# First MLP product with the two parts of an activation factor side by side in one matmul

## The chip, the cores and the metric

The kernel runs on one core of a Trainium2 chip. The metric is the device time of one execution in microseconds. Five engines work side by side, each through its own queue in order: TensorE (PE, with weight loads shown as PEld), VectorE (DVE), ScalarE (ACT), GpSimd (POOL) and SyncE (SP, which here only starts DMAs).

## What is computed

One residual layer on 512 frames of 2048 channels, all in fp32: an input projection, stick-breaking attention, a spatial gating unit, a gated merge, an output projection, and then the MLP:

```python
    for l in range(DEPTH):
        ...
        merged = jax.nn.sigmoid(gate_a) * y_a + jax.nn.sigmoid(gate_b) * y_b
        x = x + merged @ w_out[l]

        h2 = rms_norm(x, g_ff[l])
        x = x + jnp.square(jax.nn.relu(h2 @ w_ff1[l])) @ w_ff2[l]
    return x
```

The change is in `h2 @ w_ff1`, which is 512 x 2048 by 2048 x 8192.

## The kernel before

**Precision.** Each fp32 operand is split into a rounded part `hi` and a remainder `lo`, both in a format that TensorE takes in one pass. A product is the sum of three matmuls: hi by hi, hi by lo, and lo by hi (`mm3`, lines 69 to 73). `split_to` makes the parts: ACT writes hi (line 106), DVE subtracts it from the source (line 107).

**The first MLP product.** The 8192 columns go in 32 pairs of blocks of 128 columns. The first two pairs are computed plainly (bank `f`). The other 30 go through `hidden` and `strassen_columns`, which needs seven products instead of eight: y11, y21, m7, m6, y22, m4, m5. A product is 8 steps of 256 rows of the contraction, and each step is one `mm3` with 256 columns (half of the frames). Its stationary operand is a combination of weight blocks, made in `Sums.parts`: DVE sums at lines 173 (for m7), 177 (m6), 179 (y22); a GpSimd DMA that adds into a buffer at line 175 (m5). Its moving operand is one of the activation factors `hs[name, k]`, a 512-wide tile with hi in its left half and lo in its right half, held in SBUF for all pairs.

**Buffers.** The parts of a product's weights, `w_hi` and `w_lo`, are in six pieces (line 156), so those of three products fit. The products share PSUM banks of 512 columns, of which only the left 256 are used: bank 0 takes y11, then m6 on top of it, then m5 on top; bank 1 y21; bank 2 m7, then m4; bank 3 y22. Each product that goes on in a bank needs what stood there to have been read first. `slot` hands out 64 tiles of 512 columns for everything else.

**Evictions.** `evac` in `hidden` builds the four quarters a11, a12, a21, a22 of the pair's result in two `relu` tiles: ACT writes the first term of each from PSUM (y11, m7, m6, y22; line 773), DVE adds the others (y21, m4 and twice m5; line 776). Then ACT applies the ReLU (line 780), and `keep_hidden` squares (line 686), forms the factors of the second product on DVE (`m`, lines 693 to 696), splits them (`ys`) and stores them to DRAM (line 700). The second MLP product (`strassen_tokens`) reads them back.

**Order.** The code is written product by product, but a scheduler fixes each engine's order when the program is built: on every engine instructions of one product stand between those of others. On PE the products of a pair run as y11, y21, m7, y22, m6, m4, m5, before the change and after it.

Of the kernel before, what the change touches and what calls it, by code (L numbers as in the profile page):

```python
# [12 lines left out]
ALU = mybir.AluOpType  # L13
# [21 lines left out]
def tile_hybrid_layer(ctx: ExitStack, tc: tile.TileContext, x, g_mix, w_in, g_q, g_k, ln_g, ln_b,  # L35
# [4 lines left out]
    nc = tc.nc  # L40
# [12 lines left out]
    def slot(name, dt=F32, pool=slots):  # L53
        return pool.tile([P, 512], dt, name=name, tag="slot")

    def acc(name):
        return ps_acc.tile([P, 512], F32, name=name, tag="acc")
# [11 lines left out]
    def mm3(o, lh, rh, start, stop, **kw):  # L69

        nc.tensor.matmul(o, lhsT=lh[0], rhs=rh[0], start=start, stop=False, **kw)  # L71
        nc.tensor.matmul(o, lhsT=lh[0], rhs=rh[1], start=False, stop=False, **kw)  # L72
        nc.tensor.matmul(o, lhsT=lh[1], rhs=rh[0], start=False, stop=stop, **kw)  # L73
# [4 lines left out]
    def step():  # L78
        if behind:
            behind.popleft()()  # L80
# [5 lines left out]
    def weight(wap, kt, c0, w=W):  # L86

        ck = CK * W // w
        raw = state["raw"].tile([P, ck, w], F32, name="w_raw", tag="w_raw")
        state["load"] = nc.sync.dma_start(  # L90
            out=raw, in_=wap[kt * P:(kt + ck) * P, c0:c0 + w].rearrange("(k p) c -> p k c", p=P))
        hi = wpool.tile([P, ck, w], F32R, name="w_hi", tag="w_piece", bufs=6)
        nc.scalar.copy(out=hi, in_=raw)  # L93
        lo = wpool.tile([P, ck, w], F32R, name="w_lo", tag="w_piece", bufs=6)
        nc.vector.tensor_tensor(out=lo, in0=raw, in1=f32(hi), op=ALU.subtract)  # L95
        return hi, lo

    def split(src, name, scale=None, pool=slots):

        hi, lo = slot(name + "_hi", F32R, pool), slot(name + "_lo", F32R, pool)  # L100
        split_to(hi, lo, src, scale)
        return hi, lo
# [47 lines left out]
    HS = S // 2  # L150
# [38 lines left out]
    def strassen_columns(wap, c0, rhs, evac, loaded=True):  # L189

        KH = KT // 2
        blocks = {(h, c): wap[:, c0 + c * P:c0 + (c + 1) * P].rearrange("(k h p) c -> h p k c", p=P, h=2)[h]
                  for h in range(2) for c in range(2)}
        w = Sums(blocks, [state["raw"].tile([P, KH, P], F32, name="w_raw", tag="w_raw") for _ in range(6)],
                 loaded)
        banks = {}
        for name in NAMES:
            hi, lo = w.parts(name)
            b, new = BANK[name]
            if new:  # L200
                banks[b] = acc("q")
            o = banks[b][:, :HS]
            for k in range(KH):
                mm3(o, (hi[:, k, :], lo[:, k, :]), rhs[name][k], new and k == 0, k == KH - 1,
                    skip_group_check=True)
            evac(name, o)
            step()

    def strassen_tokens(wap, r0, c0, lhs, evac, between, loaded=True, after=None):
# [243 lines left out]
    for half in range(2):  # L453
# [4 lines left out]
                 lambda tb, o, v=v: v.append(split(o, "v", rstd[:, tb:tb + 1])), "v")  # L458
# [82 lines left out]
    with tc.issue_after(ref.ins):  # L541
        ws, bs = [], []
        for half in range(2):
            t = slot("ws")
            nc.sync.dma_start(out=t.rearrange("p (g j) -> p g j", g=4),
                              in_=w_sp[0, half * 4:half * 4 + 4].rearrange("g i j -> i g j"))
# [117 lines left out]
    def sides(t):  # L664
        return t[:, :HS], t[:, HS:]

    hs = {}
    order = []
    for b in range(KT):
        y = x2T[b]  # L670
        with tc.issue_after(order[b - 2].ins) if b > 1 else nullcontext():
            nc.vector.tensor_tensor(out=y, in0=y, in1=rstd_b, op=ALU.mult)
        for half in range(2):
            name = "y" + "12"[b % 2] + "12"[half]
            far = name == "y11" or name == "y21" and b // 2 < LONG - KT // 2
# [46 lines left out]
    for p in range(PLAIN):  # L722
        o = [acc("f1") for _ in range(2)]
        for kt in range(0, KT, 4):
            hi, lo = weight(w_ff1[0], kt, p * 2 * P, 2 * P)
# [3 lines left out]
            for c in range(2):  # L729
                for k in range(4):  # L730
                    a = [part[:, k, c * P:(c + 1) * P] for part in (hi, lo)]
                    for half in range(2):
                        name = "y" + "12"[k % 2] + "12"[half]
# [12 lines left out]
    class Late:  # L746
# [3 lines left out]
            self.name = name  # L750

        def __getitem__(self, k):
            return sides(hs[self.name, k])

    rhs = {name: Late(name) for name in NAMES}
    last_factors(0)
# [8 lines left out]
    def hidden(p):  # L765

        act = [slot("relu"), slot("relu")]
        a11, a12, a21, a22 = (act[c][:, half * HS:(half + 1) * HS] for c in range(2) for half in range(2))

        def evac(name, o):  # L770
            for a, sign in {"y11": [(a11, 1.0)], "m7": [(a22, 1.0)], "m6": [(a21, -1.0)],
                            "y22": [(a12, 1.0)]}.get(name, []):
                nc.scalar.activation(out=a, in_=o, func=AF.Copy, scale=sign)
            for a, op in {"y21": [(a11, ALU.add)], "m4": [(a21, ALU.add)],
                          "m5": [(a22, ALU.subtract), (a12, ALU.add)]}.get(name, []):
                state["evac"] = nc.vector.tensor_tensor(out=a, in0=a, in1=o, op=op)

        strassen_columns(w_ff1[0], p * 2 * P, rhs, evac, loaded=p < pairs - 1)
        for a in act:
            nc.scalar.activation(out=a, in_=a, func=AF.Relu)  # L780
        return act
# [11 lines left out]
    for p in range(PLAIN, pairs - 1):  # L793
        acts.append(hidden(p))
        flush()
        for _ in range(min(len(acts), 1 if p == PLAIN else 2)):
            keep_hidden(p + 1 - len(acts), acts.pop(0))
    act = hidden(pairs - 1)

    def residual(half, t, c):  # L800
# [84 lines left out]
```

## Time and profile before

| what | value |
|---|---|
| time, median of 3 runs | 2509.46 us (2508.89 to 2510.39) |
| span of the profiled execution | 2507.8 us |
| instructions in it | 35108 |
| mean granted TensorE clock | 0.997 |
| 256-column matmuls of `strassen_columns` | 3 x 1680 |
| their stretch of the span | from about 1270 to 1840 us |
| pairs in that stretch | 30 |

The profiled execution shows no time of its own beside its span. In the page's rows a group has its line, engine and operation, the tiles it writes and reads, its shape and count, the busy time and the mean duration of one, and the idle time in front of it with the instruction that ended it. In a timeline the first column is the start in us, the second the duration.

### The profile page before, as it was taken

Reading aid. Unit: us, or ns where it says so; the run is one execution under the profiler, and the core shown is the slowest. Engines: PE = TensorE matmul, PEld = TensorE weight load, DVE = VectorE, ACT = ScalarE, POOL = GpSimd, SP = SyncE. Lnnn points to the kernel's source line nnn. Section 1 sums busy time; section 2 is a strip of 40 time slices with the busy share of each in tenths; the row PEclk is TensorE's granted clock in tenths of the full one; section 3 lists DMA queues with packets and bytes.
Section 4 is the critical chain, followed back from the end, with each engine's and each line's share of the span. In section 5 each row is a group of like instructions: output and inputs, shape, how many; then the busy total and the mean of one; then the engine's idle time right before and its main releaser. Section 6 shows DMA issues by size and latency. Waiting matters only on the chain.

```text
span 2507.8 us, 35108 instructions
## 1 busy us (share of the span) xinstructions
PE 2477.8 (99%) x13658; PEld 2163.2 (86%) x13658; DVE 1603.1 (64%) x2111; ACT 1034.0 (41%) x1510; POOL 329.5 (13%) x420
## 2 busy tenths in 40 slices
PE   8999999999999999999999999999998999999999
PEld 7888888888888888888899999999996888888887
DVE  4556463223334343332698888888878989889887
ACT  5333342222322322232366666666663443333333
POOL 0212110000121010100000000000023223212210
PEclk9999999999999999999999999999999999999999
DMA  5322322333333234344269888888888887767763
GB/s 177 92 85 74 87 75 91 94 101 93 118 93 109 93 93 126 110 146 141 92 155 256 220 227 224 228 224 220 224 277 322 257 282 239 233 219 217 249 181 94
DMA packets 322584, 416.01 MB, mean 166 GB/s; under 512 B 16960, under 2 KB 176752, under 8 KB 322416
## 3 DMA queue, kind: packets, MB, share of 16 engines
q1 hardware_dynamic: 265440, 320.94, 40.1%
q0 software_dynamic: 56976, 92.82, 15.4%
q8 instruction: 107, 1.75, 0.3%
q14 instruction: 61, 0.50, 0.1%
HBM read 346.58 MB, written 67.11 MB: 165 GB/s over the span
## 4 chain that ended last, share of the span: by engine, by line
PE 94%; DMA 2%; DVE 2%; issue 1%; ACT 1%; POOL 0%; SPq 0%; DVEq 0%; POOLq 0%
PE q L72 17%; PE q L73 16%; PE q L71 16%; PE xo L73 2%; PE xo L71 2%; PE xo L72 2%; PE gb L71 2%; PE gb L73 2%; PE gb L72 2%; PE ga L71 2%; PE ga L72 2%; PE ga L73 2%; DMA w_raw<-in_w_ff_dram 1%; PE v L71 1%; PE v L73 1%; PE v L72 1%
## 5 line engine op out<-in xcount | busy, mean ns | idle before, releaser
L106 ACT CAST w_hi<-w_raw 128x1024 fp32r<-128x1024 f32 x434 | 456.7, 1052 | 586.6 <-PE q L72 536.7
L95 DVE TENSOR_TENSOR w_lo<-w_raw,w_hi 128x1024 fp32r<-128x1024 f32 x216 | 268.1, 1241 | 595.6 <-ACT w_hi L93 591.4
L107 DVE TENSOR_TENSOR w_lo<-w_raw,w_hi 128x1024 fp32r<-128x1024 f32 x434 | 530.2, 1223 | 128.1 <-ACT w_hi L106 128.1
L93 ACT CAST w_hi<-w_raw 128x1024 fp32r<-128x1024 f32 x216 | 226.6, 1049 | 663.2 <-PE ga L72 99.6
L71 PE MATMUL q<-ys,w_hi 128*128 128x256 f32 x1680 | 474.0, 283 | 0.8 <-ACT w_hi L106 0.8
L72 PE MATMUL q<-ys,w_hi 128*128 128x256 f32 x1680 | 473.9, 283 | 0.0
L73 PE MATMUL q<-ys,w_lo 128*128 128x256 f32 x1680 | 469.9, 283 | 0.0
L72 PE MATMUL q<-w_lo,ys 128*128 128x512 f32 x896 | 350.5, 391 | 10.7 <-DVE w_lo L107 10.7
L73 PE MATMUL q<-w_hi,ys 128*128 128x512 f32 x896 | 349.8, 390 | 0.0
L71 PEld LDWEIGHTS q<-ys,w_hi 128*128 128x128 f32 x1680 | 322.5, 192 | 1.0 <-ACT w_hi L106 1.0
L72 PEld LDWEIGHTS q<-ys,w_hi 128*128 128x128 f32 x1680 | 322.5, 192 | 0.0
L73 PEld LDWEIGHTS q<-ys,w_lo 128*128 128x128 f32 x1680 | 320.1, 192 | 0.0
L71 PE MATMUL q<-w_hi,ys 128*128 128x512 f32 x896 | 313.7, 390 | 0.3 <-DVE x L832 0.3
L72 PEld LDWEIGHTS q<-w_lo,ys 128*128 128x128 f32 x896 | 168.9, 189 | 47.9 <-DVE w_lo L107 13.0
L71 PEld LDWEIGHTS q<-w_hi,ys 128*128 128x128 f32 x896 | 168.5, 188 | 35.8 <-DVE x L832 0.7
L73 PEld LDWEIGHTS q<-w_hi,ys 128*128 128x128 f32 x896 | 168.9, 189 | 34.9
L175 POOL DMA_DIRECT2D w_raw<-in_w_ff_dram x57 | 79.4, 1393 | 773.7 <-DVE w_raw L173 461.3
L832 DVE TENSOR_TENSOR x<-x,q 128x512 f32<-128x512 f32 x256 | 168.0, 682 | 5.8 <-PE q L73 4.1
L788 POOL DMA_DIRECT2D ys<-store x224 | 124.6, 566 | 244.9 <-PE q L73 186.8
L71 PE MATMUL xo<-w_hi,mT_hi 128*128 128x512 f32 x256 | 100.5, 393 | 0.0
L73 PE MATMUL xo<-w_hi,mT_lo 128*128 128x512 f32 x256 | 99.9, 391 | 0.0
L72 PE MATMUL xo<-w_lo,mT_hi 128*128 128x512 f32 x256 | 99.7, 389 | 0.0
(259 smaller groups left out, 4220.6 us busy)
## 6 DMA issues: line engine op xcount, KB each, us to landing
w_raw<-in_w_ff_dram SPq DMA_DIRECT2D x256, 512.0 KB, 5.0
w_raw<-in_w_in_dram SPq DMA_DIRECT2D x144, 512.0 KB, 3.8
store<-ys SPq DMA_DIRECT2D x224, 256.0 KB, 5.0
ys<-store POOLq DMA_DIRECT2D x224, 256.0 KB, 6.1
w_raw<-in_w_ff_dram POOLq DMA_DIRECT2D x57, 512.0 KB, 6.9
w_raw<-in_w_out_dram SPq DMA_DIRECT2D x32, 512.0 KB, 3.7
w_raw<-in_w_oa_dram SPq DMA_DIRECT2D x16, 512.0 KB, 3.6
w_raw<-in_w_ob_dram SPq DMA_DIRECT2D x16, 512.0 KB, 3.7
```

Source lines behind the costliest of these rows:

```text
L71: nc.tensor.matmul(o, lhsT=lh[0], rhs=rh[0], start=start, stop=False, **kw)
L72: nc.tensor.matmul(o, lhsT=lh[0], rhs=rh[1], start=False, stop=False, **kw)
L73: nc.tensor.matmul(o, lhsT=lh[1], rhs=rh[0], start=False, stop=stop, **kw)
L93: nc.scalar.copy(out=hi, in_=raw)
L95: nc.vector.tensor_tensor(out=lo, in0=raw, in1=f32(hi), op=ALU.subtract)
L106: nc.scalar.copy(out=hi, in_=src)
L107: state["lo"] = nc.vector.tensor_tensor(out=lo, in0=src, in1=f32(hi), op=ALU.subtract)
L175: nc.gpsimd.dma_start(out=self.w21, in_=self.blocks[1, 1], accum_op=ALU.add)
L788: nc.gpsimd.dma_start(out=f32(t), in_=store[f][NAMES.index(name), p])
L832: nc.vector.tensor_tensor(out=a, in0=a, in1=o, op=op)
```

## The change

`strassen_columns` no longer calls `mm3`. A step has two matmuls: w_hi by the whole tile (hi and lo side by side, 512 columns), and w_lo by its left half (256 columns). The left half of the bank then holds hi by hi plus lo by hi, the right half hi by lo. `evac` gets the right half as `far`. ACT copies it to a `cross` tile in SBUF after every product, and GpSimd combines these copies and adds them to the quarters: eight operations of 128x256 a pair. Since a bank runs on from y11 to m6 to m5, the right half of m6's copy has y11's in it; the GpSimd steps for m4 and m5 allow for that.

```diff
-            o = banks[b][:, :HS]
+            o = banks[b]
             for k in range(KH):
-                mm3(o, (hi[:, k, :], lo[:, k, :]), rhs[name][k], new and k == 0, k == KH - 1,
-                    skip_group_check=True)
-            evac(name, o)
+                y = rhs[name][k]
+                nc.tensor.matmul(o, lhsT=hi[:, k, :], rhs=y, start=new and k == 0, stop=False,
+                                 skip_group_check=True)
+                nc.tensor.matmul(o[:, :HS], lhsT=lo[:, k, :], rhs=y[:, :HS], start=False, stop=k == KH - 1,
+                                 skip_group_check=True)
+            evac(name, o[:, :HS], o[:, HS:])
...
-        def evac(name, o):
+        cross = {}
+
+        def evac(name, o, far):
             for a, sign in {"y11": [(a11, 1.0)], "m7": [(a22, 1.0)], "m6": [(a21, -1.0)],
                             "y22": [(a12, 1.0)]}.get(name, []):
                 nc.scalar.activation(out=a, in_=o, func=AF.Copy, scale=sign)
-            for a, op in {"y21": [(a11, ALU.add)], "m4": [(a21, ALU.add)],
-                          "m5": [(a22, ALU.subtract), (a12, ALU.add)]}.get(name, []):
+            i = ("y11", "y21", "m7", "m6", "y22", "m4", "m5").index(name)
+            if i % 2 == 0:
+                cross["both"] = slot("cross")
+            r = cross[name] = cross["both"][:, i % 2 * HS:(i % 2 + 1) * HS]
+            nc.scalar.copy(out=r, in_=far)
+            for a, op, other in {"y21": [(a11, ALU.add, "y11")], "m4": [(a21, ALU.add, "m6")],
+                                 "m5": [(a22, ALU.subtract, "m7"), (a12, ALU.add, "y22")]}.get(name, []):
                 state["evac"] = nc.vector.tensor_tensor(out=a, in0=a, in1=o, op=op)
+                if name == "m4":
+                    other, r = r, cross["m6"]
+                    nc.gpsimd.tensor_tensor(out=other, in0=other, in1=r, op=ALU.subtract)
+                else:
+                    other = cross[other]
+                    nc.gpsimd.tensor_tensor(out=other, in0=other, in1=r, op=op)
+                nc.gpsimd.tensor_tensor(out=a, in0=a, in1=other, op=ALU.add)
```

The built program moves work in two places of every pair; they stand here for one pair in the middle of the stretch. A name ends in its buffer's number, and behind "waits" stand the engines or DMA queues whose semaphores the instruction waits for.

The first place is ACT around the cast of m5's weights. Before the change: w_hi_12959 is m4's, w_hi_12988 m5's, w_hi_13068 the next pair's y11; q_12810 is bank 0 (read for y11, and further down for m6), q_12872 bank 2 (m7), q_12933 bank 3 (y22).

```order
L106 CAST w_hi_12959<-w_raw_12799 128x1024 [waits DMAHW1_49,PE_49]
L106 CAST ys_12781<-m_12770 128x256 [waits DVE_49]
L106 CAST ys_12784<-m_12770 128x256 [waits DMAHW6_49]
L773 ACTIVATE relu_12794<-q_12810 128x256
L773 ACTIVATE relu_12795<-q_12872 128x256 [waits DMAHW7_49,PE_49]
L106 CAST w_hi_12988<-w_raw_12798 128x1024 [waits DMASW5_49,PE_49,Activation_49]
L773 ACTIVATE relu_12794<-q_12933 128x256 [waits PE_49]
L106 CAST w_hi_13068<-w_raw_13058 128x1024 [waits DMAHW6_49,PE_49]
```

After the change, the same stretch of ACT: w_hi_12922 is m5's cast, w_hi_13000 the next y11's; q_12779 is bank 0, q_12803 bank 1 (y21), q_12830 bank 2 (m7), q_12878 bank 3 (y22).

```order
L106 CAST w_hi_12922<-w_raw_12767 128x1024 [waits DMASW7_49,PE_49]
L106 CAST ys_12750<-m_12739 128x256 [waits DVE_49]
L106 CAST ys_12753<-m_12739 128x256 [waits DMAHW7_49]
L778 ACTIVATE relu_12763<-q_12779 128x256 [waits DMAHW0_49]
L783 COPY cross_12797<-q_12779 128x256 [waits DMAHW1_49]
L783 COPY cross_12797<-q_12803 128x256
L778 ACTIVATE relu_12764<-q_12830 128x256
L783 COPY cross_12848<-q_12830 128x256
L778 ACTIVATE relu_12763<-q_12878 128x256 [waits PE_49]
L783 COPY cross_12896<-q_12878 128x256 [waits DMAHW2_49]
L106 CAST w_hi_13000<-w_raw_12990 128x1024 [waits DMAHW4_49,PE_49]
```

The eviction of y11 stood ahead of m5's cast and now stands behind it, with the copies of y11, y21 and m7.

On PE, after the change, y22 (q_12878) ends and m6 (q_12779, on top of y11) begins like this:

```order
L205 MATMUL q_12878<-ys_8733,w_hi_12874 128x512
L207 MATMUL q_12878<-ys_8733,w_lo_12875 128x256
L205 MATMUL q_12779<-ys_9115,w_hi_12851 128x512 [waits Activation_49]
L207 MATMUL q_12779<-ys_9115,w_lo_12852 128x256
L205 MATMUL q_12779<-ys_9119,w_hi_12851 128x512
```

m6 follows y22 directly, as before, and its first matmul waits for ACT.

The second place is the end of a pair. Before the change ACT has there the cast of the next pair's m7 (w_hi_13130), both ReLUs, and the cast of the next m6 (w_hi_13161):

```order
L106 CAST w_hi_13130<-w_raw_13062 128x1024 [waits DVE_49,PE_49]
L780 ACTIVATE relu_12795<-relu_12795 128x512 [waits DVE_49]
L780 ACTIVATE relu_12794<-relu_12794 128x512 [waits DVE_49]
L686 ACTIVATE relu_12795<-relu_12795 128x512 [waits Activation_49]
L106 CAST w_hi_13161<-w_raw_13063 128x1024 [waits PE_49]
```

After it, one pair earlier in the same listing: w_hi_12851 is the next pair's m6, w_hi_12874 its y22.

```order
L106 CAST w_hi_12851<-w_raw_12770 128x1024 [waits DVE_49,PE_49]
L797 ACTIVATE relu_12539<-relu_12539 128x512 [waits Pool_49]
L689 ACTIVATE relu_12539<-relu_12539 128x512 [waits Activation_49]
L797 ACTIVATE relu_12538<-relu_12538 128x512 [waits Pool_49]
L106 CAST w_hi_12874<-w_raw_12766 128x1024 [waits DVE_49,PE_49]
```

The ReLUs waited for DVE and now wait for GpSimd, and the cast of y22 stands behind both. GpSimd, which had one DMA a pair here, now has this:

```order
L792 TENSOR_TENSOR cross_12797<-cross_12797 128x256 [waits DMAHW1_49,Activation_49]
L175 DMA w_raw_12992<-in_w_ff1_dram 128x8x128 [waits DMAHW6_49,DMASW6_49,DVE_49]
L793 TENSOR_TENSOR relu_12763<-relu_12763,cross_12797 128x256 [waits DMAHW0_49,DVE_49,Pool_49]
L789 TENSOR_TENSOR cross_12896<-cross_12896,cross_12848 128x256 [waits DMAHW2_49,Activation_49]
L793 TENSOR_TENSOR relu_12764<-relu_12764,cross_12896 128x256 [waits DVE_49,Pool_49]
L792 TENSOR_TENSOR cross_12848<-cross_12848,cross_12942 128x256 [waits Activation_49]
L792 TENSOR_TENSOR cross_12896<-cross_12896,cross_12942 128x256
L793 TENSOR_TENSOR relu_12764<-relu_12764,cross_12848 128x256 [waits DVE_49,Pool_49]
L793 TENSOR_TENSOR relu_12763<-relu_12763,cross_12896 128x256 [waits DVE_49,Pool_49]
```

The DMA's place among the adds is behind the first of them. The last four rows are those of m5: two on the copies and two that add to the quarters.

On DVE the kinds and numbers of a pair's instructions are unchanged; the weight sum L179 and the `w_lo` of the next pair's m7 stand ahead of m5's evictions.

More of the change, by code (lines that the diff above doesn't have):

```diff
@@ L752, in __getitem__ @@
         def __getitem__(self, k):
-            return sides(hs[self.name, k])
+            return hs[self.name, k]
     rhs = {name: Late(name) for name in NAMES}
```

## Prediction

> **What bounds the kernel now.** I read the page's busy table first, then the chain that ended last, then busy time by stretches.
>
> ```profile
> PE 2477.8 (99%) x13658; PEld 2163.2 (86%) x13658; DVE 1603.1 (64%) x2111; ACT 1034.0 (41%) x1510; POOL 329.5 (13%) x420
> PE 94%; DMA 2%; DVE 2%; issue 1%; ACT 1%; POOL 0%; SPq 0%; DVEq 0%; POOLq 0%
> 1400.00:1600.00 200.00, 200.00 (x1669) 200.00 (x1668) 168.50 (x248) 127.77 (x217) 15.55 (x10) 1.00 0.83 222
> 2200.00:2400.00 200.00, 200.00 (x884) 165.62 (x883) 176.83 (x190) 78.06 (x74) 47.24 (x74) 1.00 0.72 220
> ```
>
> TensorE is the bound everywhere. The columns of a stretch are PE, weight load, DVE, ACT, POOL. In the first MLP product (1400 to 1600) PE is never idle: 1669 matmuls of 256 columns in 200 us, **119.8 ns** each. In the second product (2200 to 2400) 884 matmuls of 512 columns take 226.2 ns each. So a matmul costs its columns plus some 13 ns, and a duration such as 283 ns is not its price, because matmuls overlap. A pair of column blocks is 7 products x 8 x 3 x 119.8 ns = 20.13 us. DVE is busy 168.5 of 200 us there, 17.0 us a pair; ACT 12.8 us.
>
> PE stays full because ACT and DVE are ahead of it. This is one stretch of a pair, an ACT timeline with one PE and one DVE row:
>
> ```profile
> 1503.54 1.05 ACT L106 CAST w_hi<-w_raw 128x1024 fp32r<-128x1024 f32 x1 [1.00 <-PE q L72]
> 1504.49 0.71 ACT L106 CAST ys<-m 128x256 fp32r<-128x256 f32 x2
> 1505.11 0.64 ACT L773 ACTIVATE relu<-q 128x256 f32<-128x256 f32 x2
> 1506.46 1.05 ACT L106 CAST w_hi<-w_raw 128x1024 fp32r<-128x1024 f32 x1 [0.71 <-ACT relu L773]
> ...
> 1506.34 0.28 PE L71 MATMUL q<-ys,w_hi 128*128 128x256 f32 x1
> ...
> 1504.63 1.23 DVE L107 TENSOR_TENSOR w_lo<-w_raw,w_hi 128x1024 fp32r<-128x1024 f32 x1 [0.39 <-ACT w_hi L106]
> ```
>
> The six piece buffers hold hi and lo of three products, so each cast waits until the product three back is finished: casts come one product (2.88 us) apart. Here y22 ends on PE and m6 begins at 1506.34, and the cast of m5 follows at 1506.46, 0.12 us later. The eviction of y11 (1505.11) is done before that, so m6, which goes on in y11's bank, starts without a gap.
>
> **The change, term by term, for one pair.**
>
> *Matmuls.* Of three matmuls of 256 columns (359.4 ns) come one of 512 and one of 256, 226.2 + 119.8 = 346.0 ns. No column is saved, only one fixed part: 13.4 ns x 56 = **-0.75 us** a pair, a product takes 2.77 us. Alternating 512 and 256 is not in the trace. The nearest mixed stream is this one:
>
> ```profile
> 789.37 0.34 PE L581 MATMUL mix<-wsp,vn_hi 128*128 128x256 f32 x1
> 789.54 0.22 PE L583 MATMUL mix<-wsp,vn_lo 128*128 128x128 f32 x1
> 789.60 0.34 PE L581 MATMUL mix<-wsp,vn_hi 128*128 128x256 f32 x1
> ```
>
> It takes 230 ns for 384 columns; at 512 columns per 226.2 ns the columns alone would be 160, so up to 70 ns lie beside them. With 70 for 768 columns a step would take 390 ns, +1.7 us a pair. I take -0.75, since both widths hold 13 ns in long streams and the weight load before a 512 again lies under 256 columns; the ends are -0.75 and +1.7.
>
> *A new wait of PE for ACT (m6).* Every product now has a second copy on ACT, and the built order puts both copies of y11 behind the cast of m5 (the order after, ACT: CAST w_hi_12922, two ys casts, relu<-q_12779, COPY cross<-q_12779). By the counts in the built program that cast waits for the last w_hi matmul of y22, and the first matmul of m6 (PE: q_12779<-ys_9115) waits for that COPY, because it writes into the bank that the COPY reads. So m6 can't start before y22 has ended and cast, two ys casts, eviction and copy are through. The same five stand in the rows above: 1503.54 to 1505.75 = 2.21 us. With the 0.12 ahead of it and 0.1 for the release it is **+2.4 us** a pair; nothing covers it, PE has only m6 next. Between 2.1 (no latencies) and 2.8 (ys casts late on DVE).
>
> *GpSimd and DVE on the same data (y22).* GpSimd gets eight adds of 128x256 a pair.
>
> ```profile
> L424 POOL TENSOR_TENSOR beta<-beta,past x32: 460/676/1432, 157.7 to 368.2; 128x128 f32<-128x128 f32 x32
> L604 POOL TENSOR_TENSOR merged<-merged,merged_a x16: 1276/1288/2273, 880.9 to 1037.4; 128x512 f32<-128x512 f32 x16
> ...
> 884.25 1.29 POOL L604 TENSOR_TENSOR merged<-merged,merged_a 128x512 f32<-128x512 f32 x1 [2.06 <-DVE merged L603]
> 884.38 2.24 DVE L95 TENSOR_TENSOR w_lo<-w_raw,w_hi 128x1024 fp32r<-128x1024 f32 x1 [0.21 <-ACT w_hi L93]
> ...
> 832.53 1.22 DVE L95 TENSOR_TENSOR w_lo<-w_raw,w_hi 128x1024 fp32r<-128x1024 f32 x1
> 832.75 2.14 POOL L588 TENSOR_TENSOR smix<-smix,u 128x512 f32<-128x512 f32 x1 [6.77 <-DVE smix L587]
> ```
>
> Undisturbed, 128 columns take 0.46 us and 512 take 1.29; the line between them gives 0.74 for 256 (estimate; ends 0.46 and 1.29). The last four rows are the point: a DVE subtraction begun under a GpSimd add took 2.24 instead of 1.23 us, 1.01 of the 1.16 us they overlapped; the other way round GpSimd took 2.14 instead of 1.29. Whoever comes second waits, and this holds for every DVE operation with two inputs in SBUF: w_lo, the weight sums, m and ys. Those with an input from PSUM (the evictions) go on. So eight adds put 8 x (0.74 - 0.15) = 4.7 us on DVE's 17.0, 21.7 us a pair, which is more than PE's 19.4 alone.
>
> The Trainium skill says the same in "SBUF — State Buffer", section "Who interferes with whom": a Vector instruction with two SBUF inputs and a GpSimd instruction that reads SBUF exclude each other, and the second is blocked until the first finishes. By that rule each add would cost 0.74, 5.9 us a pair; the rows show 0.15 less each.
>
> Where does it meet PE? The ReLU of a pair now waits for GpSimd's last two adds, and ACT's cast of the next pair's y22 stands behind both ReLUs (order after, end of a pair). ReLU and square take 0.6 us each.
>
> ```profile
> L780 ACT ACTIVATE relu<-relu 128x512 f32<-128x512 f32 x60 | 34.4, 621 | 0.1
> L686 ACT ACTIVATE relu<-relu 128x512 f32<-128x512 f32 x62 | 38.3, 622 | 0.0
> ```
>
> DVE's long operations follow each other 1.14 us apart:
>
> ```profile
> 1506.77 1.22 DVE L173 TENSOR_TENSOR w_raw<-w_raw 128x1024 f32<-128x1024 f32 x1
> 1507.91 1.22 DVE L107 TENSOR_TENSOR w_lo<-w_raw,w_hi 128x1024 fp32r<-128x1024 f32 x1
> ```
>
> I count from m5's end on PE. The cast of m7 and the copy of m5 take ACT to 1.4. GpSimd and DVE then alternate: DVE's sum L179 to 1.3, GpSimd's add for m4 to 2.0, w_lo of m7 to 3.0, GpSimd's two subtractions to 4.5, w_lo of m6 (which asked while the second ran) to 5.45, GpSimd's two adds to 6.2 and 6.9. ACT: first ReLU 6.2 to 6.8, square to 7.4, second ReLU to 8.0, cast of y22 to 9.0; DVE's w_lo to 10.25. PE has y11, y21 and m7 to do (3 x 2.77 = 8.3) and needs w_lo of y22 for its second matmul at 8.55: **+1.7 us** a pair. If nobody had to wait, the adds would end at 4.5, and w_lo at 7.9: no cost. With adds of 1.29 us the four behind m5 add 2.2: 3.9 us. I take 1.7, as the line between two sizes is near both rows.
>
> *Costs that I put at nothing.* The seven extra ACT copies, at 0.32 us as the evictions above, make 15 us of ACT in a pair of over 22. GpSimd's weight DMA stands behind one add now, but its sum is needed only for the next m5, some 18 us on.
>
> ```profile
> 1508.59 1.55 POOL L175 DMA_DIRECT2D w_raw<-in_w_ff_dram  x1 [18.61 <-DVE w_raw L173]
> ```
>
> Its issue of 1.55 us comes before the first add and far from the four at the end of a pair. Evictions on DVE are as before. The order of the first three pairs differs (DVE still makes input factors there): only the -0.75 each.
>
> **Sum.** -0.75 + 2.4 + 1.7 = +3.35 us, a period of 23.5 us for 20.13. Of 30 pairs 27 have this order: 27 x 3.35 - 3 x 0.75 = +88 us. The profiled span of 2507.8 becomes 2596; the span is 1.7 us under the median 2509.46, so the time is **2598 us**.
>
> **Rivals.**
> 1. *Only the wait at m6.* GpSimd's adds find DVE's idle time (3.1 us a pair before, more with the new wait), and y22 is ready. For it: the waits themselves give DVE room. Against it: the adds fall on the stretch where L179 and three w_lo stand close. 27 x 1.65 - 2 = +42: 2552 us.
> 2. *The port decides.* The adds take nearer to 1.29 us, and y22 is 3.9 us late: 27 x 5.55 - 2 = +148: 2657 us.
> 3. *The mixed stream is no gain.* 390 ns a step as in the mixing of the spatial unit: 1680 x (390 - 346) = +74 on the sum: 2672 us. Against it: there a 256 loads under only 128 columns.
> 4. *Faster.* PE meets no wait, and the 13.4 ns x 1680 remain: -22.6, 2487 us. One thing decides: y11's copies would have to be done when y22 ends, 2.4 us earlier, as they are in the rows of before; that is so if the cast ahead of them is released one product sooner, by m7. The built counts speak against it.
>
> **How the numbers follow.** Forecast 0.62 (2575 to 2620), rival 1 0.15, rival 2 0.13, rival 3 0.05, rival 4 0.05. The range 2545 to 2645 takes the forecast, rival 1 and half of rival 2, 0.83. A measurement here tells 0.2% (5 us) from no change: faster 0.04, the same 0.01 (rival 4 with a shorter wait), slower 0.95.
>
> **What would show it.** In the stretch 1400 to 1600 PE should be some 83% busy, with two gaps per pair: 2.4 us in front of m6, released by ACT's COPY, and one in front of y22's first w_lo matmul, released by DVE, about 1.7. DVE's w_lo mean should rise over its 1.22, GpSimd's adds should lie well over 0.74 in the mean. A pair every 20 us or less, or no wait for COPY, would make me wrong; a y22 gap of nothing or 4 us would put rivals 1 or 2 in its place, a step of 390 ns in a full stretch rival 3.

## The result and the profile after

| | before | after |
|---|---|---|
| time, median of 5 runs each | 2509.46 us (2508.30 to 2510.39) | 2615.42 us (2614.08 to 2621.18) |
| ratio | | 1.0425, 95% interval 1.0413 to 1.0438 |
| profiled execution: span | 2507.8 us | 2619.5 us |
| mean granted TensorE clock | 0.997 | 0.989 |

The change makes the kernel 4.2% slower, 106 us. The forecast was 2598 us, with 2545 to 2645 as the range. The profiled execution is the slowest of the five (2621.2 us). (The table of the kernel before puts the end of the 256-column stretch at about 1840 us; the last of these matmuls ends at 1878 in that trace.)

These lines answer to those of before. From the page: busy time, the chain that ended last, and two groups; from the windows: the two stretches (PE, weight load, DVE, ACT, POOL, then clock).

```profile
PE 2502.7 (96%) x11978; PEld 2086.6 (80%) x11978; DVE 1637.6 (63%) x2111; ACT 1091.5 (42%) x1720; POOL 672.5 (26%) x660
...
PE 78%; POOL 7%; ACT 6%; issue 5%; DVE 4%; DMA 1%; SPq 0%; DVEq 0%; POOLq 0%; ACTq 0%
...
L107 DVE TENSOR_TENSOR w_lo<-w_raw,w_hi 128x1024 fp32r<-128x1024 f32 x434 | 549.3, 1267 | 231.4 <-ACT w_hi L106 227.2
...
L793 POOL TENSOR_TENSOR relu<-relu,cross 128x256 f32<-128x256 f32 x120 | 178.3, 1496 | 5.7 <-DVE relu L786 3.1
```
```profile
1400.00:1600.00 200.00, 171.75 (x931) 143.12 (x930) 150.91 (x215) 126.91 (x252) 108.79 (x73) 0.99 0.70 191
2200.00:2400.00 200.00, 200.00 (x884) 165.62 (x883) 175.76 (x189) 77.62 (x74) 57.05 (x92) 1.00 0.79 246
```

The second product (2200 to 2400) is as it was. In the first, PE is busy 86% where it was never idle, and the chain leaves PE for POOL, ACT and DVE. What PE waits for stands in the list of waits (total us, times, longest):

```profile
PE q L205 <- ACT cross L783: 58.5, 27, 2.2
PE q L207 <- DVE w_lo L107: 25.6, 29, 2.6
...
PE q L205 <- ACT w_hi L106: 5.7, 28, 0.4
```

One pair on PE, in order of time: the last matmul of m7, y22's first and second, y22's last, m6's first and second, and y22's first of the next pair.

```profile
1591.43 0.28 PE L207 MATMUL q<-ys,w_lo 128*128 128x256 f32 x1
1592.05 0.50 PE L205 MATMUL q<-ys,w_hi 128*128 128x512 f32 x1 [0.34 <-ACT w_hi L106]
1593.31 0.38 PE L207 MATMUL q<-ys,w_lo 128*128 128x256 f32 x1 [0.76 <-DVE w_lo L107]
...
1595.85 0.28 PE L207 MATMUL q<-ys,w_lo 128*128 128x256 f32 x1
1598.30 0.50 PE L205 MATMUL q<-ys,w_hi 128*128 128x512 f32 x1 [2.17 <-ACT cross L783]
1598.64 0.28 PE L207 MATMUL q<-ys,w_lo 128*128 128x256 f32 x1
...
1615.68 0.50 PE L205 MATMUL q<-ys,w_hi 128*128 128x512 f32 x1 [0.17 <-ACT w_hi L106]
```

A pair takes 1615.68 - 1592.05 = 23.63 us; the forecast was 23.5. In a full stretch a 512 begins about 0.11 us behind a 256, and a 256 about 0.23 behind a 512. So y22 loses (0.62 - 0.11) + (1.26 - 0.23) = 1.54 us, and m6 2.45 - 0.11 = 2.34 us. What is left, 19.75 us, is 56 steps of about 352 ns.

On ACT, in the same pair, stands what the two waits hang on:

```profile
1589.24 0.64 ACT L797 ACTIVATE relu<-relu 128x512 f32<-128x512 f32 x1 [2.10 <-POOL relu L793]
...
1590.44 0.62 ACT L797 ACTIVATE relu<-relu 128x512 f32<-128x512 f32 x1
1590.96 1.03 ACT L106 CAST w_hi<-w_raw 128x1024 fp32r<-128x1024 f32 x1
...
1596.05 1.04 ACT L106 CAST w_hi<-w_raw 128x1024 fp32r<-128x1024 f32 x1 [0.34 <-PE q L205]
1597.00 0.71 ACT L106 CAST ys<-m 128x256 fp32r<-128x256 f32 x2
1597.61 0.37 ACT L778 ACTIVATE relu<-q 128x256 f32<-128x256 f32 x1
1597.89 0.64 ACT L783 COPY cross<-q 128x256 f32<-128x256 f32 x2
```

The first three rows are y22's: the first ReLU waits for GpSimd, and y22's cast (1590.96) stands behind the second ReLU. The other four are m6's: m5's cast begins when y22 has ended, and behind it come two `ys` casts, y11's eviction and its far copy, the first of the two copies in the last row. m6 begins at 1598.30.

What no line of the forecast has is this, the m6 of the next pair:

```profile
1621.93 0.80 PE L205 MATMUL q<-ys,w_hi 128*128 128x512 f32 x1 [2.17 <-ACT cross L783]
1622.52 0.42 PE L207 MATMUL q<-ys,w_lo 128*128 128x256 f32 x1
1622.74 0.63 PE L205 MATMUL q<-ys,w_hi 128*128 128x512 f32 x1
...
1625.30 0.41 PE L205 MATMUL q<-ys,w_hi 128*128 128x512 f32 x1
```
```profile
1622.00:1625.00 3.00, 3.00 (x9) 2.61 (x10) 3.00 (x6) 1.25 (x5) 2.77 (x2) 0.50 0.81 308
1626.00:1629.00 3.00, 3.00 (x19) 2.66 (x18) 1.23 (x1) 1.59 (x3) 0.86 (x2) 1.00 0.72 84
```

The first fence is PE's timeline, the second two windows of 3 us. For 3.4 us a step takes 0.64 us and the granted clock (third number from the end) is 0.50; then it is 1.00 again. The m6 after this one comes 25.07 us later, at 1647.00, the next again 23.63 us on: 1.4 us for each halved stretch of the clock.

### The profile page after: what moved, and what is told of

Same layout as the page of the kernel before. It is cut to its first block, busy times and chain, and to the rows that moved or that the text cites. A ratio compares the mean times of both kernels' runs of the same rounds, so it can differ in the third digit from the quotient of the medians.

```text
span 2619.5 us, 32397 instructions
## 1 busy us (share of the span) xinstructions
PE 2502.7 (96%) x11978; PEld 2086.6 (80%) x11978; DVE 1637.6 (63%) x2111; ACT 1091.5 (42%) x1720; POOL 672.5 (26%) x660
## 3 DMA queue, kind: packets, MB, share of 16 engines
q8 instruction: 94, 1.54, 0.2%
## 4 chain that ended last, share of the span: by engine, by line
PE 78%; POOL 7%; ACT 6%; issue 5%; DVE 4%; DMA 1%; SPq 0%; DVEq 0%; POOLq 0%; ACTq 0%
PE q L71 8%; PE q L72 8%; PE q L73 8%; PE q L205 6%; POOL relu L793 3%; PE q L207 3%; PE xo L73 2%; PE xo L71 2%; PE xo L72 2%; PE gb L71 2%; PE gb L73 2%; PE gb L72 2%; PE ga L71 2%; PE ga L73 2%; PE ga L72 2%
## 5 line engine op out<-in xcount | busy, mean ns | idle before, releaser
L107 DVE TENSOR_TENSOR w_lo<-w_raw,w_hi 128x1024 fp32r<-128x1024 f32 x434 | 549.3, 1267 | 231.4 <-ACT w_hi L106 227.2
L205 PE MATMUL q<-ys,w_hi 128*128 128x512 f32 x1680 | 611.3, 407 | 64.3 <-ACT cross L783 58.5
L95 DVE TENSOR_TENSOR w_lo<-w_raw,w_hi 128x1024 fp32r<-128x1024 f32 x216 | 267.9, 1240 | 596.4 <-ACT w_hi L93 592.4
L205 PEld LDWEIGHTS q<-ys,w_hi 128*128 128x128 f32 x1680 | 320.7, 192 | 154.1 <-ACT cross L783 67.3
L792 POOL TENSOR_TENSOR cross<-cross 128x256 f32<-128x256 f32 x90 | 139.1, 1559 | 269.9 <-ACT cross L783 233.2
L793 POOL TENSOR_TENSOR relu<-relu,cross 128x256 f32<-128x256 f32 x120 | 178.3, 1496 | 5.7 <-DVE relu L786 3.1
```

Source lines behind the costliest of these rows:

```text
L107: state["lo"] = nc.vector.tensor_tensor(out=lo, in0=src, in1=f32(hi), op=ALU.subtract)
L205: nc.tensor.matmul(o, lhsT=hi[:, k, :], rhs=y, start=new and k == 0, stop=False, skip_group_check=True)
L792: nc.gpsimd.tensor_tensor(out=other, in0=other, in1=r, op=op)
L793: nc.gpsimd.tensor_tensor(out=a, in0=a, in1=other, op=ALU.add)
```

## The experiments

All times are medians; the kernel before had 2508.7 to 2510.4 us beside them. "Adds" are the eight 128x256 operations of a pair that bring the far half in. The runs are told by their source edits; where the built order (the order in which a program was built for each engine) moves more than the edit says, the text says so.

| run | what differs from the changed kernel | us | ratio to before, 95% interval |
|---|---|---|---|
| e4_matmuls_alone | wide matmuls only, no copies, no adds | 2498.0 | 0.9927 to 0.9960 |
| e2_no_adds | no adds | 2501.9 | 0.9952 to 0.9978 |
| e1_copy_first | y11's far copy ahead of m5's cast | 2613.1 | 1.0396 to 1.0427 |
| e5_adds_on_dve | adds on VectorE | 2614.2 | 1.0400 to 1.0431 |
| e12_dve_copy_first | e1 and e5 together | 2578.5 | 1.0256 to 1.0290 |
| e6_keep_after_y11 | square and split after y11 of the next pair | 2585.3 | 1.0286 to 1.0316 |
| e7_relu_after_y22 | ReLU too, after y22 of the next pair | 2541.3 | 1.0111 to 1.0141 |
| e8_dve_relu_after_y22 | e7, adds on VectorE | 2512.9 | 1.0004 to 1.0023 |
| e9_last_pair_at_once | e8, the last but one pair at once | 2512.9 | 1.0004 to 1.0021 |
| e10_gap_filled | e5, idle matmuls ahead of m6 | 2581.2 | 1.0268 to 1.0300 |
| e11_wide_in_middle | e8 for pairs 5 to 28, the rest as before | 2504.9 | 0.9970 to 0.9989 |

### What the matmuls save, and what the additions cost in all

Both runs leave the product of the high weight part and the low activation part out of the sum. e4: the `cross` tiles, their copies and all GpSimd operations are taken out of `evac`.

```diff
-            if i % 2 == 0:
-                cross["both"] = slot("cross")
-            r = cross[name] = cross["both"][:, i % 2 * HS:(i % 2 + 1) * HS]
-            nc.scalar.copy(out=r, in_=far)
...
-                    nc.gpsimd.tensor_tensor(out=other, in0=other, in1=r, op=op)
-                nc.gpsimd.tensor_tensor(out=a, in0=a, in1=other, op=ALU.add)
```

> Only the wide matmuls are left of the change: no copy of the far half and no add (the product of the high weight part and the low activation part is left out of the sum). Theory: the stream alone, 351 ns a step for 359.4, gives 2509 - 1680 x 0.008 = 2496 us; by the prediction's 346 ns it would be 2487 us; by 390 ns (the rival that the mixed stream is no gain) 2560 us.

e2: only the GpSimd operations are taken out (the last two lines of that diff, and the one for m4).

> The eight GpSimd adds of a pair are left out, so the product of the high weight part and the low activation part is computed and copied, but missing from the sum; the built order then also has y11's copies ahead of m5's cast. Theory: without the adds neither the wait at m6 nor the one at y22 is left, and the matmuls save 8 ns a step of two: 2509 - 1680 x 0.008 = 2496 us, with TensorE at 99% busy again. Rival (the seven extra copies on ScalarE hold PE as well): above 2509 us.

One window of each, of before, of e4, of e2:

```profile
1600.00:1800.00 200.00, 200.00 (x1669) 200.00 (x1669) 169.63 (x250) 127.49 (x219) 15.53 (x10) 1.00 0.84 224
```
```profile
1600.00:1800.00 200.00, 200.00 (x1135) 173.83 (x1134) 171.43 (x255) 130.21 (x223) 15.53 (x10) 1.00 0.84 227
```
```profile
1600.00:1800.00 200.00, 200.00 (x1137) 173.74 (x1136) 170.82 (x257) 146.01 (x298) 15.53 (x10) 1.00 0.84 227
```

PE is never idle in any of them. 1669 matmuls in threes are 359.5 ns a step, 1135 in pairs 352.4: the wide form saves 7 ns a step, 1680 x 7 = 12 us, and e4 is 11.8 us faster. The seven extra ACT copies (ACT 130 to 146 us) cost next to nothing: e2's 3.8 us more are spent in small waits of the first pairs and where the second product begins (waits for w_lo of 4.31 and 8.78 us; in e4 they are 1.92, 7.38 and 0.62). So all of the loss, 2615 less 2502 = 113 us, hangs on the adds and on the order that they bring. In e2's built order y22's cast stands behind both ReLUs, as in the changed kernel, and y22 does not wait: that place costs nothing as long as the ReLUs are not late. Both expectations held, e4's to 2 us and e2's to 6.

### The two waits, one at a time

e1 puts m5's cast behind y11's far copy:

```diff
-            hi, lo = w.parts(name)
+            with tc.issue_after(state["copied"].ins) if name == "m5" else nullcontext():
+                hi, lo = w.parts(name)
...
-            nc.scalar.copy(out=r, in_=far)
+            copied = nc.scalar.copy(out=r, in_=far)
+            if name == "y11":
+                state["copied"] = copied
```

> The far copy of y11 is made to stand ahead of m5's cast on ScalarE; nothing else is changed. Theory: the wait at m6 (2.34 us from start to start in each regular pair of the changed kernel) goes, and with it the halved clock that followed it now and then. What is left is y22's lateness, some 1.5 us a pair, because its chain (m5's copy, GpSimd's last adds, ReLU, cast, w_lo) starts at m5's end and has three products to run in: 2509 + 27 x (1.5 - 0.45) + about 8 for the first pairs = 2545 us. Rival A (GpSimd and VectorE exclude each other and together need 21.7 us a pair, so whatever is freed at m6 comes back at y22): 27 x 1.6 + 8 on 2509, about 2560 us, with y22's wait over 2 us. Rival B (the wait at m6 was only cover for y22, all comes back): about 2610 us.

By its time rival B, 2613 us, though not by its mechanism: next to nothing moved to y22 (some 0.2 us), the wait stayed at m6 and only fell from 2.17 to 1.95 us. ACT's timeline in e1 says why:

```profile
1367.18 0.63 ACT L800 ACTIVATE relu<-relu 128x512 f32<-128x512 f32 x1 [2.10 <-POOL relu L796]
1367.85 0.63 ACT L690 ACTIVATE relu<-relu 128x512 f32<-128x512 f32 x1
...
1372.38 0.40 ACT L106 CAST ys<-m 128x256 fp32r<-128x256 f32 x1
1373.24 0.41 ACT L106 CAST ys<-m 128x256 fp32r<-128x256 f32 x1 [0.46 <-DVE m L698]
1374.71 0.71 ACT L106 CAST ys<-m 128x256 fp32r<-128x256 f32 x2 [1.06 <-DVE m L699]
1375.33 0.38 ACT L779 ACTIVATE relu<-q 128x256 f32<-128x256 f32 x1
1375.61 0.64 ACT L784 COPY cross<-q 128x256 f32<-128x256 f32 x2
```

m5's cast is gone from this place, but y11's eviction (1375.33) still stands behind the casts of the pair before. These wait for DVE's `m`. It needs the square, which needs the ReLU (1367.18), which waits for GpSimd; and on DVE it stands behind `w_lo` of y22, which is late by the same ReLUs, and of another product (begun at 1369.97 and 1373.13). m6 begins at 1376.02, when the copy is done. The wait has two legs, and the second ends 0.2 us ahead of the first.

e5 leaves the source order and moves the adds:

```diff
-                    nc.gpsimd.tensor_tensor(out=other, in0=other, in1=r, op=op)
-                nc.gpsimd.tensor_tensor(out=a, in0=a, in1=other, op=ALU.add)
+                    nc.vector.tensor_tensor(out=other, in0=other, in1=r, op=op)
+                nc.vector.tensor_tensor(out=a, in0=a, in1=other, op=ALU.add)
```

> The eight adds of a pair run on VectorE instead of GpSimd; the built order on ScalarE still has y11's copies behind m5's cast. Theory: VectorE needs 17.0 + 8 x some 0.37 = 20.0 us a pair and nobody excludes it, so y22 is no longer late, while the wait at m6 stays at 2.3 us: 27 x (2.34 - 0.45) = +51, 2560 us, and up to 10 more if the clock still drops after that wait. Rival (the lateness of y22 is the chain behind m5, whoever adds): y22 waits 1.5 us as before, about 2605 us.

By its time the rival won, by its waits the theory: y22 waits no more in the regular pairs, m6 waits 2.17 us as before, and a pair without a halved clock takes 22.20 us (m6 at 1412.67 and 1434.87). But after 22 of the 26 waits from 1388.94 on the clock is halved, and such a pair takes 1.2 to 1.5 us more (1434.87 to 1458.29 is 23.42); the first pairs had single waits of 4.39 and 7.26 us for the copies besides. So the equal time is made of other things than the changed kernel's.

The theory's reason for y22 isn't shown, because the edit moved more than the adds. In the built order of e5 y22's cast stands ahead of both ReLUs, on ACT:

```profile
1427.02 1.05 ACT L106 CAST w_hi<-w_raw 128x1024 fp32r<-128x1024 f32 x1 [1.83 <-PE q L205]
1427.98 1.15 ACT L797 ACTIVATE relu<-relu 128x512 f32<-128x512 f32 x2
```

So it waits neither for the ReLUs nor for the last adds. The adds themselves end only 0.65 us earlier than in the changed kernel: 6.15 us behind the pair's first matmul (1421.12) against 6.80 (1583.11). By these numbers most of what y22 gained came from the cast's place, not from the faster engine; no run has the adds on VectorE with the cast where it was.

e12 does both single edits, by the two diffs above:

> The adds on VectorE, and y11's far copy ahead of m5's cast on ScalarE: both single edits that brought nothing (2613 and 2614 us) together. Theory (two legs under the wait at m6): without m5's cast, 1.05 us, the wait is what the casts of the pair before leave; with the adds on VectorE their rows run without a gap from the ReLU to y11's copy, so the wait falls by about 1.0 to 1.1 or 1.2 us, not to nothing; a wait of that size halves the clock seldom or never. A pair takes some 21.1 us: 2510 + 26 x 1.0 + some 20 for the first pairs and the end = 2556 us. Rival A (m5's cast alone held m6 once nobody is late behind GpSimd): no wait, 2515 us. Rival B (as with GpSimd, the second leg takes over whole): 2.0 us, 2600 us.

Between the theory and rival B. Together the two edits, worth 2 and 1 us alone, are worth 37 us: y22 is in time (its cast stands ahead of the ReLUs, as in e5), m6 waits 1.74 to 1.84 us, a pair takes 21.6 us, with a halved clock behind 8 of the 25 waits from 1382.75 on. That the wait would fall by the 1.05 us of m5's cast was wrong: with the adds on VectorE the second leg ends 0.3 to 0.4 us ahead of the first, with GpSimd's 0.2.

### Moving the work behind the ReLU

e6 calls `keep_hidden` one step later, when y11 of the next pair has been evicted:

```diff
-            keep_hidden(p + 1 - len(acts), acts.pop(0))
+            behind.append(lambda q=p + 1 - len(acts), act=acts.pop(0): keep_hidden(q, act))
```

> As the changed kernel, but the squaring and splitting of the pair before (keep_hidden) is called after y11 of the next pair has been evicted, so on ScalarE y11's copies stand ahead of that work and of m5's cast. In the run with the copy of y11 ahead of m5's cast alone, the wait at m6 stayed 1.95 us because the casts of the pair before, late since its ReLU waits for GpSimd, stood ahead of it too. Theory (two legs under the wait at m6, both taken away here): the wait at m6 is gone or below 0.3 us (m7's copies, still behind that work, may hold m4 by some tenths), the halved clock with it; y22 is still 1.5 us late since its cast stands behind both ReLUs: 2509 + 27 x (1.5 + 0.2 - 0.45) + 8 = 2551 us. Rival (GpSimd and VectorE cannot do a pair in less than 23.4 us): about 2612 us, with the wait at another product.

Neither. m6 was in time, and y22 too, with the adds still on GpSimd: in the built order m6 now stands ahead of y22 on PE (so it does in e7 and e8), which gives y22's cast one product more. That cast ends at 1419.06, when the fourth product, begun at 1418.44, is under way. But then PE waits mostly 1.7 to 2.3 us for a COPY in every pair (2.00 us at 1426.25). By the built order this is m7's copy, ahead of m4, now the first eviction behind the four `ys` casts. The wait moved by one product.

e7 moves the ReLU along, in the source to the step behind y22; in the built order the first ReLU stands behind y11's copy and ahead of y22's cast:

```diff
+        late = [lambda act=acts[-1]: relu(act)]
         for _ in range(min(len(acts), 1 if p == PLAIN else 2)):
-            keep_hidden(p + 1 - len(acts), acts.pop(0))
+            late.append(lambda q=p + 1 - len(acts), act=acts.pop(0): keep_hidden(q, act))
+        behind.extend([lambda: None] * 3 + [lambda late=late: [f() for f in late]])
```

> As the changed kernel, but ReLU, squaring and splitting of a pair are called after y22 of the next pair, so neither y22's cast nor y11's copies stand behind work that waits for GpSimd's adds. The adds stay on GpSimd. Theory (the waits came from the order of work on ScalarE behind the late ReLU, not from a lack of time on any engine): no wait at m6 and none at y22; the bound is then VectorE with what GpSimd excludes, 17.0 us less 1.6 us of evictions from PSUM plus eight adds of 0.6 to 0.74, 20.2 to 21.3 us a pair, if it can't be hidden: 2500 to 2545 us, 2525 as the middle. Rival (exclusion decides, whatever the order): 2550 us and above, TensorE waiting for w_lo at many products.

2541 us, in the upper part of the theory's range. No wait for a COPY is left in the regular pairs; what remains are waits of 0.2 to 0.8 us for w_lo and w_hi, 21.07 us a pair (1433.39 to 1454.46). e8 is e7 with the adds on VectorE, by the diff of e5:

> As the run before it (ReLU, squaring and splitting after y22 of the next pair), with the eight adds on VectorE. Theory: VectorE needs 17.0 + 8 x 0.42 = 20.4 us a pair and becomes the bound by a little: 2509 + 27 x (20.4 - 20.13) = 2516 us, with short waits for w_lo and no halved clock. Rival (GpSimd's adds cost VectorE no more than its own would): the same time as the run before it.

The windows of e7 and of e8:

```profile
1600.00:1800.00 200.00, 191.48 (x1055) 160.72 (x1053) 170.39 (x236) 138.39 (x279) 125.76 (x85) 1.00 0.78 207
```
```profile
1600.00:1800.00 200.00, 200.00 (x1139) 173.92 (x1138) 195.19 (x340) 147.55 (x296) 15.53 (x10) 1.00 0.85 229
```

With the same source order and the same PE order GpSimd's adds leave PE idle 4% and VectorE's leave it full, though DVE is then at 195 of 200: 28 us between the two runs. They are the price of the engine and of the order together, which no run here takes apart: in e8 the ReLUs stand behind the casts of y22 and m4, in e7 ahead of them, and ACT waits there for GpSimd (4.47 us up to 1599.94). What makes GpSimd slow is that it and DVE shut each other out, as this stretch of the changed kernel shows (POOL, then DVE):

```profile
1605.58 1.51 POOL L789 TENSOR_TENSOR cross<-cross 128x256 f32<-128x256 f32 x1 [1.29 <-ACT cross L783]
1607.17 1.60 POOL L793 TENSOR_TENSOR relu<-relu,cross 128x256 f32<-128x256 f32 x1
```
```profile
1605.27 1.23 DVE L107 TENSOR_TENSOR w_lo<-w_raw,w_hi 128x1024 fp32r<-128x1024 f32 x1 [1.55 <-ACT w_hi L106]
1606.41 0.41 DVE L786 TENSOR_TENSOR relu<-relu,q 128x256 f32<-128x256 f32 x1
1606.74 1.43 DVE L179 TENSOR_TENSOR w_raw<-w_raw 128x1024 f32<-128x1024 f32 x1
1608.28 1.58 DVE L107 TENSOR_TENSOR w_lo<-w_raw,w_hi 128x1024 fp32r<-128x1024 f32 x1
```

An add on GpSimd takes 0.73 us where nothing is in its way (the shortest of 120). The one that began under the w_lo of 1605.27 lasted 1.51 us; DVE's sum of 1606.74 that began under it took 1.43 for 1.22; the next add 1.60. The eviction from PSUM (1606.41) kept its 0.41.

### The halved clock

e10 is e5 with TensorE kept busy where it waits, between y22 and m6:

```diff
+            if name == "y22":
+                idle = aux("idle")
+                with tc.issue_after(last.ins):
+                    for _ in range(9):
+                        nc.tensor.matmul(idle, lhsT=rhs["m6"][0][:, :P], rhs=rhs["m6"][0], start=True, stop=True)
```

> As the run with the adds on VectorE and ScalarE's order as in the changed kernel (TensorE waits 2.17 us at m6 in every pair, and in 21 of 26 pairs its clock is halved for some 3 us within 2 us behind that wait), but nine matmuls of 512 columns (9 x 226 ns = 2.03 us) into a bank that nobody reads stand between y22 and m6, so TensorE is busy where it waited. Theory (the halved clock comes from the idle time at m6): no halved clock in the regular pairs; a pair falls from 23.4 us in the mean to 22.2, 26 x 1.2 = 31 us less, about 2580 us. Rival (the clock drops for another reason, or the matmuls delay m6): 2614 us or more.

2581 us, 33 less than e5: work that nobody needs makes the kernel faster. The same window of e5 and of e10:

```profile
1600.00:1800.00 200.00, 182.60 (x967) 156.90 (x966) 165.25 (x282) 120.54 (x241) 13.67 (x9) 0.94 0.71 189
```
```profile
1600.00:1800.00 200.00, 199.09 (x1100) 169.58 (x1099) 174.69 (x300) 131.09 (x264) 14.00 (x9) 1.00 0.76 203
```

The granted clock goes from 0.94 to 1.00, and no halved stretch is left in it. A pair takes 21.9 to 22.3 us, as a pair of e5 without a halved clock; the first four pairs take what they took (101.8 us for 101.6). So idle time at m6 does halve the clock, and it costs 1.2 to 1.5 us each time, over half of what the wait itself costs.

### Can the gain be kept?

e8 holds 19.7 us a pair (1139 matmuls in 200 us are 351 ns a step, 56 steps) and still ends 3.6 us behind the kernel before, 2509.3 us beside it. It loses two waits of about 2 us in the first pairs, and most where the second product begins:

```profile
1922.56 0.79 PE L72 MATMUL q<-w_lo,ys 128*128 128x512 f32 x1 [9.73 <-DVE w_lo L107]
```
```profile
1912.87 1.23 DVE L173 TENSOR_TENSOR w_raw<-w_raw 128x1024 f32<-128x1024 f32 x1 [6.29 <-DMA w_raw<-in_w_ff_dram]
1920.15 1.23 DVE L181 TENSOR_TENSOR w_raw<-w_raw 128x1024 f32<-128x1024 f32 x1 [6.05 <-DMA w_raw<-in_w_ff_dram]
1921.29 1.22 DVE L107 TENSOR_TENSOR w_lo<-w_raw,w_hi 128x1024 fp32r<-128x1024 f32 x1
```

The first fence is PE's, the second DVE's timeline: the weights come late. In the kernel before that wait is 1.66 us.

e9 takes the last pair but one out of the delay, e11 (below, its new condition and the branch that the narrow pairs take) all but pairs 5 to 28:

```diff
-        behind.extend([lambda: None] * 3 + [lambda late=late: [f() for f in late]])
+        if p < pairs - 2:
+            behind.extend([lambda: None] * 3 + [lambda late=late: [f() for f in late]])
+        else:
+            for f in late:
+                f()
```

> As the run with the adds on VectorE and ReLU, squaring and splitting after y22 of the next pair, but the last pair but one is squared and split at once, as before. In that run TensorE ran without a gap at 19.7 us a pair and lost its gain at the end of the first product: 2.35 us at 1880.88 and 9.73 us at 1922.56, with some 3 us of halved clock behind it, where the kernel before waits 1.66 us at the same place. Theory (the gain of the matmuls, 7 to 8 ns a step, is there and was spent at that end): about 2502 us, faster than the kernel before by 0.3%. Rival (the same work meets the same end wherever it is put): 2513 us.

A miss: the wait there went down to 4.66 us, and others came in the last pairs (2.25 us for w_lo at 1863.28, 4.93 for a COPY at 1871.07).

```diff
+    def wide(p):
+        return 5 <= p < pairs - 3
...
+                if not wide:
+                    mm3(o[:, :HS], (hi[:, k, :], lo[:, k, :]), sides(y), new and k == 0, k == KH - 1,
+                        skip_group_check=True)
+                    continue
```

> A mixture: pairs 5 to 28 have the wide matmuls with the adds on VectorE and ReLU, squaring and splitting after y22 of the next pair; pairs 2 to 4 and 29 to 31 have the three narrow matmuls and the order of the kernel before, since in the two runs with that order the gain of the regular pairs was lost in the first pairs (two waits of 2 us for y11's copies and a halved clock) and at the change to the second product. Theory: 24 pairs x 0.40 to 0.45 us = 10 us less and nothing given back, 2499 to 2501 us, faster than the kernel before by 0.4%. Rival (what is gained is given back at the ends, wherever the wide pairs stop): 2509 to 2513 us.

Half of what was expected: 2504.9 us, 0.1% to 0.3% faster than the kernel before, the best that has the whole sum. Single waits of 0.3 to 1.0 us are left at some copies (0.95 us at 1738.54), and the wait at the start of the second product is 9.40 us at one place (1893.76) where the kernel before has 7.60. What decides when the weights of the second product arrive was not tried.

## Why the prediction was right, and where it wasn't

Forecast was 2598 us, measured 2615: inside the range, on the forecast's side of every rival. By its steps:

- **Matmuls, -0.75 us a pair.** The sign held, the size didn't: 7 ns a step in e4 and e2 instead of 13.4, -0.4 us a pair. Two widths in turn cost 352 ns where the sum of the two long streams gives 346. Rival 3 (390 ns) is out.
- **Wait at m6, +2.4 us.** Measured 2.34 from start to start, with 27 such waits in the list. As a price it was right, and the rows behind it are those that the prediction named (cast at 1596.05 to copy at 1597.89). As a cause it was half of it: the prediction let the wait start with m5's cast and took the `ys` casts of the pair before to be late only in its upper bound. e1 took m5's cast away and got 0.2 us, because y11's eviction stands behind the late ReLU's work as well. So the price per wait was right, but it could not be had back by removing its named cause.
- **GpSimd against DVE, y22 1.7 us late.** Measured 1.54, of which 0.51 in front of the first w_hi matmul and 1.03 in front of the first w_lo matmul. The mechanism is in the traces as told: counted from m5's end (y11 follows at 1583.11), ReLU at 6.1 us for 6.2, end of y22's cast at 8.9 for 9.0, end of its w_lo at 10.2 for 10.25; and an add alone takes 0.73 us for the estimate of 0.74. Without late ReLUs (e2), with the cast ahead of them (e5) or with a product more to run in (e6) y22 does not wait. What GpSimd costs over VectorE with the order held still no run shows; e7 against e8 has 28 us for engine and order together.
- **Sum.** A regular pair without a halved clock takes 23.6 us for 23.5. That it came so near is in part luck: 0.35 us too much gain on the matmuls against 0.06 and 0.16 us too much on the waits. The missing 23 us (span 2619.5 for 2596; 17 by the medians) are two things that had no term. From y22 of one pair at 1376.70 to that of the 25th after it at 1974.10 are 597.4 us, 10 more than 25 x 23.5; the clock is halved in five of these pairs, 5 x 1.4 = 7 us. Another 13 us lie in the first four pairs, which take 94.7 us for 81.6: the first three were put at -0.75 each because their order differs, but w_lo is late in the second, third and fourth (PE waits 1.39, 2.58 and 1.90 us), with the clock halved in the last two of these. The end costs nothing: from the last of these matmuls to the end of the span are 629.0 us, 629.8 before.
- **What would show it.** PE 86% busy in 1400 to 1600 for 83%, both waits with the releasers named, w_lo's mean 1.27 us over 1.22, GpSimd's adds 1.50 us over 0.74: all as told.

What the runs show of the cause: the adds make the ReLU late, and on ACT, which runs in order, the ReLU and all that hangs on it stand ahead of y22's cast and of y11's copies for the next pair. m6 may not touch y11's bank until these copies are done, and m5's cast, which has nothing to do with the adds, stands ahead of them too. So m6's wait has two legs of nearly the same length, and with one taken away the other holds.

## What to carry to other kernels

When two waits come from one late producer, removing either can show nothing; ask what else stands ahead of the same instruction on its in-order engine, and move the whole late group (e7, e8), not one member of it (e1, e6). Look at the built order before you credit an edit: moving the adds (e5) also moved a cast, and moving the square (e6) also swapped two products on PE. A saving of 7 ns a step is small beside one PE wait of 2 us a pair, and a bank that is written again makes every new reader of it a possible wait. Count a wait of TensorE for more than its length where the clock can fall behind it.

## What the hardware showed that was not expected

TensorE's granted clock fell to 0.50 for 3.41 us after waits of only 1.7 to 2.2 us, and not after each: behind 22 of 26 in e5 (2.17 us), behind 8 of 25 in e12 (1.74 to 1.84 us), behind 6 of the 26 at m6 from 1382.99 on in the changed kernel (2.17 to 2.18 us). In e5 the fall comes up to 1.5 us behind the wait, in work.

The traces show which waits are spared. In each of them all falls lie on one grid of 3.413 us (in e5 for instance 1434.83, 1458.72 and 1482.61, seven steps apart). Two steps of that grid in e5 with the step that follows each, the first pair around the wait that ends at 1412.67, the second around the one that ends at 1434.87:

```profile
1410.93:1414.34 3.41, 1.67 (x9) 1.49 (x10) 3.41 (x6) 3.05 (x10) 0.78 (x1) 1.00 0.85 322
1414.34:1417.76 3.42, 3.42 (x22) 2.96 (x21) 3.42 (x8) 1.59 (x3) 0.77 (x1) 1.00 0.72 142
```
```profile
1431.42:1434.83 3.41, 1.28 (x8) 0.86 (x6) 3.41 (x7) 3.41 (x10) 0.00 (x0) 1.00 0.73 243
1434.83:1438.24 3.41, 3.37 (x10) 2.89 (x11) 3.41 (x8) 1.36 (x5) 1.56 (x1) 0.50 0.75 279
```

Both waits are 2.17 us long. The second lies almost whole in one step, PE is idle for 2.13 of its 3.41 us, and the clock is halved in the next; the first is cut by a grid line, 1.74 us are idle in one step, and it is spared. So it is with all four that e5 spares. From 1380 to 1990 us in the traces of this case no step with less than 1.7 us idle (by the rows of PE) was followed by a fall from the full clock, and each with more than 1.9 us was. This is read off the traces; no run shifted a wait on the grid.

The Trainium skill ("TensorE: Matmul & The Clock Gate", section "Part 1: The HAM clock gate (the "warmup" mystery)") has the clock go to half after an idle window of about 3.4 us and back after as long a busy one. The way back agrees with these traces; the idle time needed does not, a step that is idle for little over half does it here.
